# The last six column tiles of an output projection, split by halves of the tokens

## The chip, the cores and the metric

One Trainium2 chip, one of its cores. The metric is device microseconds from the start to the end of one execution. The kernel before was run three times on the chip; a further execution of it was recorded by the hardware profiler, and all rows below are from that one.

## The reference, cut to what matters

Two layers of an encoder over 512 tokens and 16 meta tokens (528 in all), width 2048. Layer 0 is attention, layer 1 gated linear attention. Each layer normalises its input, mixes, projects back to 2048, normalises again and adds the result to its input:

```
h = concat(meta, x)                                  # 528 x 2048
for i in 0, 1:
    y = rmsnorm(h, pre_norm[i])
    y = mixer_i(y, w_in[i], ...) @ w_out[i]          # gated outputs x w_out
    h = h + rmsnorm(y, post_norm[i])
return h[:, 16:]
```

The change is in the passage from layer 0 to layer 1: the product with `w_out[0]`, the norm of its result, the addition to `h`, the norm before layer 1 and the first product with `w_in[1]`.

## The kernel before

All activations are feature-major: 16 blocks k of 128 features, on partitions, by 528 tokens. The tokens are cut into two halves of 264 (HALVES). Float32 products are made in three passes of float32r: each operand is kept as a high part and the rest (`uh` and `ul` for activations, `whi` and `wlo` for weights), and `three` (lines 153 to 156) issues high x high, low x high, high x low.

**Weights.** `weights` (lines 143 to 151) fetches one unit: a DMA of 512 KB into `wraw` on SP's queue (line 149), a cast into `whi` on ACT (line 131) and a subtraction into `wlo` on DVE (line 132), the last two called the cast and the split here. `wraw` has two buffers, `whi` and `wlo` three each. A unit of `w_out` is 8 blocks k by 128 columns. The split of a unit frees its `wraw` buffer, and the last product with it frees its `whi` and `wlo`.

**Output projection.** `project` (lines 158 to 169) makes one column tile m of 128 columns: it fetches two units, and for each half of the tokens runs all 16 k, 48 products of 264 columns, and calls `evac`. Tiles 0 and 1 are made earlier; the loop over m = 2 to 15 makes the others. `evac` calls `squares` (lines 601 to 610): ACT writes `hs[m]` (line 602) and the square of the result (line 607), POOL adds the squares into `acc` (line 609). Behind the last tile's half, `mean_rsqrt` (lines 617 to 623) sums `acc` over partitions with TensorE (line 621), DVE makes mean and epsilon (line 622), ACT the reciprocal root (lines 135, 136) into `r0`.

**Residual step.** `residual(k, a, b)` (lines 625 to 639) fetches the layer's input `h0` by DMA on SP's queue (line 628), multiplies `hs[k]` by `r0` on DVE (630), adds `h0` on DVE for even k and on POOL for odd k (631), and splits the sum times the next norm's weight into `uh` (ACT, 632) and `ul` (DVE, 633). ACT squares it (638) and POOL adds the square to `acc` (639). It overwrites the gated outputs in `uh` and `ul`, so it may only begin for a half when all 16 column tiles of that half are made. For 264 tokens an even k takes 3 instructions on DVE and 1 on POOL, an odd k 2 and 2, so both together 5 and 3 (k = 0 has no line 639).

**First product of layer 1.** `group` (lines 171 to 188) makes two column tiles of `w_in[1]` for both halves at once, with k outermost. The first `halves` of k go by the first half of the tokens, then by the second, the others with both. Before the products of a k, `low_rank` (lines 650 to 663) issues the next residual step (`ahead`), the products `plr` (lines 652, 653), and, when the second half is there, four transposes of `hs[k]` into a PSUM tile `ht` (line 659), a copy of it on ACT into `hb` (line 661) and a DMA of `hb` (line 662). `ht` has one buffer for even k and one for odd k.

**Order.** The program writes the instructions in the order of the calls; a clock object `clk` places side work (`clk.after`, `clk.drive`) among the products by an estimated time. The framework then orders each engine's queue by itself, with weights pulled ahead (`high_priority(400)`). Each engine takes its queue strictly in order.

Of the kernel before, what the change touches and what calls it, by code (L numbers as in the profile page):

```python
# [19 lines left out]
P = 128  # L20
# [18 lines left out]
class Clock:  # L39
    """Order of emission: main steps advance the time, events run when it has come."""  # L40
# [42 lines left out]
def hybrid_encoder(  # L83
# [42 lines left out]
    # the activations of both layers and their gated outputs, feature-major, in two parts  # L126
# [31 lines left out]
    def project(src, c0, parts, evac, last_k=None):  # L158
        """One column tile of a projection: all of k for one part of the tokens, then for the next."""
        ws = [weights(src[:, k0:k0 + 8, c0:c0 + P]) for k0 in (0, 8)]  # L160
        for a, b in parts:
            ps = ps_p.tile([P, 512], F32, tag="pp", name="pp")[:, :b - a]
            for k in range(KT):
                wh, wl = ws[k // 8]
                three(ps, wh[:, k % 8], wl[:, k % 8], k, a, b, k == 0, k == KT - 1)
                clk.step(3 * (b - a + 7) / 2400)
                if last_k and (a, b) == parts[-1]:
                    last_k(k)
            evac(ps, a, b)

    def group(srcs, accs, extra, ahead=AHEAD, halves=0, units=None):
        """Several column tiles side by side, k outermost; the first of k by halves of the tokens, if asked."""
# [22 lines left out]
    # ======== layer 0: attention ========  # L195
# [10 lines left out]
    def take(wcol):  # L206
        """Evacuation of one q or k head: w * x and the squares."""
# [33 lines left out]
    def qk_tiles():  # L241
        kh = wk.tile([P, T], F32R, tag="kh", name="kh")
        kl = wk.tile([P, T], F32R, tag="kl", name="kl")
        # two heads' queries: real 0, meta 0, meta 1, real 1
# [107 lines left out]
    # per-token sums of squares: the norm as a column, and along the tokens  # L352
# [179 lines left out]
    # the output projection starts on the heads that are there  # L532
# [49 lines left out]
    # low-rank gate weights: the down-projection as columns [f hi, b hi, f lo, b lo] from multiples of 32,  # L582
    # the up-projections as rows [hi, lo, hi] against the inputs' rows [hi, hi, lo]
# [41 lines left out]
    def residual(k, a, b):  # L625
        if a == 0:
            h0s[k] = t2.tile([P, T], F32, tag="h0", name="h0", bufs=6)
            nc.sync.dma_start(out=h0s[k], in_=h0_d[k])
        h, hi = hs[k][:, a:b], uh[:, k, a:b]
        V.tensor_tensor(h, h, r0[:, a:b], op=ALU.mult)  # L630
        (G if k % 2 else V).tensor_tensor(h, h, h0s[k][:, a:b], op=ALU.add)
# [32 lines left out]
    def evac(ps, a, b):  # L664
        sq = squares(m, ps, a, b)
        if m == KT - 1:
            if a == 0:
                clk.after(1.5, lambda: mean_rsqrt(r0, [acc[:, a:b], sq], a, b))
                clk.after(2.5, lambda: ahead(NA))
            else:  # L670
                clk.after(0.9, lambda: mean_rsqrt(r0, [acc[:, a:b], sq], a, b))

    NA, NB = 2, 6
    h0s = {}
    tasks = [(k, a, b) for a, b in HALVES for k in range(NB)] + [(k, 0, T) for k in range(NB, KT)]
# [6 lines left out]
    for m in range(2, KT):  # L682
        project(w_out0, m * P, HALVES, evac)

# [30 lines left out]
    # ======== layer 1: gated linear attention ========  # L715
# [9 lines left out]
    # masks over a diagonal block, keys on partitions: forward j <= i, backward j > i  # L725
# [20 lines left out]
    def gates(h):  # L746
# [23 lines left out]
        # references of the key blocks, plus and minus, with the gate's 1/16  # L770
# [7 lines left out]
    def decayed(src, b, cc, j, sgn, c, n, what):  # L778
        """hi/lo of src * exp(sgn * (b - c_j) / 16) over n columns from c, both key tiles."""
# [145 lines left out]
    # the gated outputs come back for the output projection, and its norm's weights  # L925
# [43 lines left out]
    # ======== output projection, token-major, and the last residual ========  # L969
    def token_group(n, banks, on_k=None, evac=None):  # L970
        """512 columns of all token tiles, which end one after another if they are to be finished here."""
# [99 lines left out]
```

## Time and profile before

| | |
|---|---|
| median of 3 runs | 1826.01 us (1825.46 to 1826.07) |
| span of the profiled execution | 1825.2 us |
| the same above or below the median of the runs | 0.8 us below |
| PE busy | 1784.4 us, 98% |
| DVE busy | 1014.2 us, 56% |
| ACT busy | 892.9 us, 49% |
| POOL busy | 202.5 us, 11% |

The profile gives, for the execution that it recorded, the span from the first to the last instruction; a time around it is not shown, so the 0.8 us are taken to lie around it. PE is TensorE's products, PEld its weight loads, DVE is VectorE, ACT ScalarE, POOL GpSimd, SP the queue from which most DMAs are issued. The shares are means over the whole span; the passage that the change touches is about 130 us of it.

### The profile page before, as it was taken

How to read it: one execution, taken by the hardware profiler on the slowest of the kernel's cores; microseconds unless marked ns; L12 is line 12 of the kernel's file. 1: busy time of each engine (PE TensorE's matmuls, PEld its weight loads, DVE VectorE, ACT ScalarE, POOL GpSimd, SP SyncE). 2: the span in 40 equal slices, each digit the busy share in tenths (PEclk: the TensorE clock that was granted, in tenths of full speed). 3: DMA queues.
4: the chain of work that ended last, by engine and by line, in shares of the span. 5: the costliest groups of instructions: out<-in, count | busy, mean ns of one | idle time of the engine just before them, and what ended most of it. 6: DMA issues, size and time to landing. Idle time of an engine off the chain costs nothing.

```text
span 1825.2 us, 31789 instructions
## 1 busy us (share of the span) xinstructions
PE 1784.4 (98%) x12825; PEld 1683.3 (92%) x12825; DVE 1014.2 (56%) x1941; ACT 892.9 (49%) x1835; POOL 202.5 (11%) x212
## 2 busy tenths in 40 slices
PE   8899999999999999999987999999999999999997
PEld 7899999999999999999987898998999899988886
DVE  5776665656565657622258475656456555654224
ACT  5555444454454544533245586556447455743221
POOL 2211111111111110211137000000000000000000
PEclk9999999999999999999998999999999999999999
DMA  8323232333223242633335323232232323434323
GB/s 266 106 59 82 82 88 85 93 85 88 83 87 93 81 120 76 185 93 93 93 88 163 87 72 89 83 82 82 81 93 80 84 87 92 134 116 172 94 92 127
DMA packets 264595, 184.22 MB, mean 101 GB/s; under 512 B 8108, under 2 KB 240112, under 8 KB 263920
## 3 DMA queue, kind: packets, MB, share of 16 engines
q1 hardware_dynamic: 259808, 165.78, 31.5%
q0 software_dynamic: 4640, 16.42, 2.5%
q8 instruction: 100, 1.64, 0.4%
q14 instruction: 47, 0.39, 0.1%
HBM read 156.03 MB, written 19.64 MB: 96 GB/s over the span
## 4 chain that ended last, share of the span: by engine, by line
PE 92%; DVE 3%; ACT 1%; DMA 1%; POOL 1%; issue 1%; SPq 0%; DVEq 0%; POOLq 0%; ACTq 0%
PE pp L154 22%; PE pp L156 22%; PE pp L155 22%; PE f L985 2%; PE f L983 2%; PE f L984 2%; PE pT L453 2%; PE s L434 1%; PE s L435 1%; PE s L436 1%; PE o L863 1%; PE o L862 1%; PE o L861 1%; PE o L474 1%; PE o L473 1%
## 5 line engine op out<-in xcount | busy, mean ns | idle before, releaser
L154 PE MATMUL pp<-uh,whi 128*128 128x264 f32 (+1 forms) x3072 | 927.4, 302 | 2.5 <-ACT uh L308 2.1
L156 PE MATMUL pp<-uh,wlo 128*128 128x264 f32 (+1 forms) x3072 | 916.4, 298 | 0.0
L155 PE MATMUL pp<-ul,whi 128*128 128x264 f32 (+1 forms) x3072 | 915.1, 298 | 0.7 <-DVE ul L309 0.7
L154 PEld LDWEIGHTS pp<-uh,whi 128*128 128x128 f32 x3072 | 578.5, 188 | 21.1 <-ACT uh L308 2.5
L155 PEld LDWEIGHTS pp<-ul,whi 128*128 128x128 f32 x3072 | 578.8, 188 | 16.9 <-DVE ul L309 1.2
L156 PEld LDWEIGHTS pp<-uh,wlo 128*128 128x128 f32 x3072 | 578.5, 188 | 16.2
L132 DVE TENSOR_TENSOR wlo<-wraw,whi 128x1024 fp32r<-128x1024 f32 x256 | 316.0, 1235 | 385.8 <-ACT whi L131 380.7
L131 ACT CAST whi<-wraw 128x1024 fp32r<-128x1024 f32 x256 | 267.7, 1047 | 416.1 <-PE pp L155 297.1
L443 ACT ACTIVATE pn<-s,mx 128x528 f32<-128x528 f32 (+1 forms) x72 | 50.4, 699 | 88.4 <-DVE mx L440 65.0
L985 PE MATMUL f<-whi,ul 128*128 128x512 f32 x192 | 75.6, 394 | 0.0
L983 PE MATMUL f<-whi,uh 128*128 128x512 f32 x192 | 75.5, 393 | 0.0
L984 PE MATMUL f<-wlo,uh 128*128 128x512 f32 x192 | 75.3, 392 | 0.0
L225 POOL TENSOR_TENSOR qw<-qw,cos 128x528 f32<-128x528 f32 x24 | 31.9, 1328 | 372.2 <-DMA qs<-qw 347.7
L888 POOL DMA_DIRECT2D og_d<-og x24 | 12.9, 545 | 486.8 <-DVE og L886 486.8
L439 DVE TENSOR_REDUCE mx<-s 128x1 f32<-128x528 f32 (+1 forms) x72 | 50.8, 705 | 18.5 <-PE s L436 17.3
L235 DVE TENSOR_TENSOR qw<-qw,qs 128x528 f32<-128x528 f32 x24 | 17.0, 708 | 60.0 <-POOL qs L226 60.0
L458 DVE TENSOR_TENSOR pl<-pT,ph 128x512 fp32r<-128x512 f32 (+1 forms) x80 | 47.4, 593 | 4.8 <-ACT ph L457 3.8
L457 ACT CAST ph<-pT 128x512 fp32r<-128x512 f32 (+1 forms) x80 | 40.7, 508 | 16.5 <-PE pT L453 10.4
L428 POOL TENSOR_TENSOR gs<-gs,gr 128x528 f32<-128x528 f32 x16 | 21.2, 1323 | 222.3 <-ACT gs L141 205.4
L984 PEld LDWEIGHTS f<-wlo,uh 128*128 128x128 f32 x192 | 36.1, 188 | 8.3
L985 PEld LDWEIGHTS f<-whi,ul 128*128 128x128 f32 x192 | 36.1, 188 | 8.3
L983 PEld LDWEIGHTS f<-whi,uh 128*128 128x128 f32 x192 | 36.1, 188 | 8.1
(306 smaller groups left out, 2743.2 us busy)
## 6 DMA issues: line engine op xcount, KB each, us to landing
wraw<-in_gla_w_in_dram SPq DMA_DIRECT2D x96, 512.0 KB, 3.9
wraw<-in_attn_w_in_dram SPq DMA_DIRECT2D x95, 512.0 KB, 4.1
wraw<-in_attn_w_out_dram SPq DMA_DIRECT2D x32, 512.0 KB, 3.9
wraw<-in_gla_w_out_dram SPq DMA_DIRECT2D x32, 512.0 KB, 3.8
qs<-qw SPq DMA_DIRECT2D x96, 66.0 KB, 3.0
h<-h_d SPq DMA_DIRECT2D x16, 264.0 KB, 3.8
h_d<-h POOLq DMA_DIRECT2D x16, 256.0 KB, 2.9
h_d<-hb SPq DMA_DIRECT2D x16, 256.0 KB, 3.1
```

What stands on the lines that cost most here:

```text
L131: A.copy(hi, src)
L132: V.tensor_tensor(lo, src, hi.bitcast(F32), op=ALU.subtract)
L154: PE.matmul(ps, wh, uh[:, k, a:b], start=first, stop=False)
L155: PE.matmul(ps, wh, ul[:, k, a:b], start=False, stop=False)
L156: PE.matmul(ps, wl, uh[:, k, a:b], start=False, stop=last)
L439: V.reduce_max(mx, s, axis=AX.XY)
L443: A.activation(pn[:, :T].rearrange("p (a b) -> p a b", a=2), s, AF.Exp, bias=mx, scale=SCALE, accum_out=sm)
L457: A.copy(ph[:, :, c:c + m], pt[:, :, qc:qc + m])
L458: V.tensor_tensor(pl[:, :, c:c + m], pt[:, :, qc:qc + m], ph[:, :, c:c + m].bitcast(F32), op=ALU.subtract)
L983: PE.matmul(ps, uh[:, k, ts], wh[:, kk], start=(k == 0), stop=False)
L984: PE.matmul(ps, uh[:, k, ts], wl[:, kk], start=False, stop=False)
L985: PE.matmul(ps, ul[:, k, ts], wh[:, kk], start=False, stop=(k == KT - 1))
```

## The change

Tiles 2 to 9 are made as before. Tiles 10 to 15 are made for the first half of the tokens, one after the other, and then for the second half, so each of their weights is fetched and split twice. When the first half's mean is there, a side task issues the 16 residual steps of the first half, one every 2.0 us of the clock, beside the products of the second half. The 16 residual steps of the second half are issued from `group`, whose first 10 k (6 before) go by halves. `h0` is fetched by half (132 KB into 8 buffers) and no longer whole (264 KB into 6). Comments and some docstrings are gone as well.

```diff
     def residual(k, a, b):
-        if a == 0:
-            h0s[k] = t2.tile([P, T], F32, tag="h0", name="h0", bufs=6)
-            nc.sync.dma_start(out=h0s[k], in_=h0_d[k])
+        h0 = t2.tile([P, HALF], F32, tag="h0", name="h0", bufs=8)
+        nc.sync.dma_start(out=h0, in_=h0_d[k][:, a:b])
...
-        (G if k % 2 else V).tensor_tensor(h, h, h0s[k][:, a:b], op=ALU.add)
+        (G if k % 2 else V).tensor_tensor(h, h, h0, op=ALU.add)
...
-                clk.after(2.5, lambda: ahead(NA))
+                clk.after(3.0, lambda: side.append(clk.drive(residuals(KT))))
...
-    NA, NB = 2, 6
-    h0s = {}
-    tasks = [(k, a, b) for a, b in HALVES for k in range(NB)] + [(k, 0, T) for k in range(NB, KT)]
+    TAIL, NB = 6, 10
+    side = []
+    tasks = [(k, a, b) for a, b in HALVES for k in range(KT)]
...
+    def residuals(n):
+        for _ in range(n):
+            ahead(1)
+            yield 2.0
+
-    for m in range(2, KT):
+    for m in range(2, KT - TAIL):
         project(w_out0, m * P, HALVES, evac)
+    for part in HALVES:
+        for m in range(KT - TAIL, KT):
+            project(w_out0, m * P, (part,), evac)
+    clk.finish(*side)
```

From line 628 on the line numbers of the two kernels differ by one: line 630 of before is 629 of the change, 631 is 630, 633 is 632, 661 is 660.

**VectorE, at the last tiles of the projection.** `wlo` is a unit's split, `r0` the first half's mean, lines 630 to 633 the residual steps; the number behind `h` is k. Before, with the splits of the last tile's units and of the group's first ones:

```order
L132 TENSOR_TENSOR wlo_11506<-wraw_11504,whi_11505 128x1024
L622 TENSOR_SCALAR r0_9785<-ssq_11446 128x264
L630 TENSOR_TENSOR h0_9768<-h0_9768,r0_9785 128x264
L630 TENSOR_TENSOR h1_9769<-h1_9769,r0_9785 128x264
L631 TENSOR_TENSOR h0_9768<-h0_9768,h0_11461 128x264
L132 TENSOR_TENSOR wlo_11586<-wraw_11584,whi_11585 128x1024
L633 SCALAR_TENSOR_TENSOR ul_88<-h0_9768,cols_85,uh_87 128x264
L633 SCALAR_TENSOR_TENSOR ul_88<-h1_9769,cols_85,uh_87 128x264
L630 TENSOR_TENSOR h2_9770<-h2_9770,r0_9785 128x264
L630 TENSOR_TENSOR h3_9771<-h3_9771,r0_9785 128x264
L631 TENSOR_TENSOR h2_9770<-h2_9770,h0_11510 128x264
L132 TENSOR_TENSOR wlo_11828<-wraw_11826,whi_11827 128x1024
```

With the change, where `wlo_11254` and `wlo_11260` are the two units of tile 11 for the second half, and `wlo_11337` the first of tile 12:

```order
L132 TENSOR_TENSOR wlo_11254<-wraw_11252,whi_11253 128x1024
L622 TENSOR_SCALAR r0_9785<-ssq_11193 128x264
L629 TENSOR_TENSOR h0_9768<-h0_9768,r0_9785 128x264
L629 TENSOR_TENSOR h1_9769<-h1_9769,r0_9785 128x264
L630 TENSOR_TENSOR h0_9768<-h0_9768,h0_11211 128x264
L132 TENSOR_TENSOR wlo_11260<-wraw_11258,whi_11259 128x1024
L632 SCALAR_TENSOR_TENSOR ul_88<-h0_9768,cols_85,uh_87 128x264
L632 SCALAR_TENSOR_TENSOR ul_88<-h1_9769,cols_85,uh_87 128x264
L629 TENSOR_TENSOR h2_9770<-h2_9770,r0_9785 128x264
L629 TENSOR_TENSOR h3_9771<-h3_9771,r0_9785 128x264
L630 TENSOR_TENSOR h2_9770<-h2_9770,h0_11280 128x264
L132 TENSOR_TENSOR wlo_11337<-wraw_11335,whi_11336 128x1024
```

The residual steps of the first half have moved from ahead of the splits of `w_in[1]` to ahead of those of `w_out`'s last tiles. Between one split and the next stand five of their instructions, for two steps; this goes on through eight splits, `wlo_11260` to `wlo_11613`.

**ScalarE, in the group.** Lines 632 (631 with the change) and 638 (637) are residual steps; `hb` are the copies of the transposes. Before, the three copies are those of k = 9, 10 and 11:

```order
L632 ACTIVATE uh_87<-h12_9780,cols_85 128x528
L638 ACTIVATE sq1_11904<-h12_9780 128x528
L661 COPY hb_11883<-ht_11878 128x512
L632 ACTIVATE uh_87<-h13_9781,cols_85 128x528
L638 ACTIVATE sq1_11937<-h13_9781 128x528
L632 ACTIVATE uh_87<-h14_9782,cols_85 128x528
L638 ACTIVATE sq1_11976<-h14_9782 128x528
L661 COPY hb_11916<-ht_11911 128x512
L632 ACTIVATE uh_87<-h15_9783,cols_85 128x528
L638 ACTIVATE sq1_12009<-h15_9783 128x528
L661 COPY hb_11949<-ht_11944 128x512
```

With the change they are those of k = 2, 3, 4, 5 and 6, where `whi_12157` is the group's last unit and `whi_12276` the first of the projection behind it:

```order
L660 COPY hb_11960<-ht_11955 128x512
L131 CAST whi_12157<-wraw_12156 128x1024
L631 ACTIVATE uh_87<-h13_9781,cols_85 128x264
L637 ACTIVATE sq1_11975<-h13_9781 128x264
L660 COPY hb_11985<-ht_11980 128x512
L631 ACTIVATE uh_87<-h14_9782,cols_85 128x264
L637 ACTIVATE sq1_12000<-h14_9782 128x264
L660 COPY hb_12010<-ht_12005 128x512
L631 ACTIVATE uh_87<-h15_9783,cols_85 128x264
L637 ACTIVATE sq1_12025<-h15_9783 128x264
L660 COPY hb_12035<-ht_12030 128x512
L131 CAST whi_12276<-wraw_12275 128x1024
```

The copies have moved back against the residual steps: behind the last step stood the copy of k = 11, now it is that of k = 5. The first copy, of k = 0, stands behind the step of k = 9 with the change, and behind that of k = 2 before.

Elsewhere the order between casts and evacuations is as it was: the last evacuation of the second half (`h15`) stands on ScalarE behind the cast of the group's third unit in both kernels.

## Rows read from the trace of the kernel before

**Rows 1.** The page's head: the span, and of each engine the busy time, its share of the span and the instructions.

```profile
span 1825.2 us, 31789 instructions
PE 1784.4 (98%) x12825; PEld 1683.3 (92%) x12825; DVE 1014.2 (56%) x1941; ACT 892.9 (49%) x1835; POOL 202.5 (11%) x212
```

**Rows 2.** Busy time of each engine by stretches (from:to, its length, then PE, PEld, DVE, ACT and POOL busy with their instructions, the granted clock, the share of the DMA engines, GB/s). The first stretch is in the output projection, the others from the first residual step to the last, and the whole of `group`.

```profile
880.00:920.00 40.00, 40.00 (x332) 40.00 (x331) 9.27 (x8) 13.32 (x22) 5.66 (x6) 1.00 0.31 87
939.90:943.50 3.60, 3.33 (x25) 2.92 (x25) 3.54 (x7) 2.74 (x7) 1.03 (x2) 1.00 0.00 0
943.50:948.60 5.10, 3.63 (x26) 3.29 (x26) 5.10 (x8) 2.91 (x7) 3.66 (x4) 1.00 0.47 125
948.90:963.50 14.60, 10.68 (x80) 9.46 (x79) 14.60 (x24) 10.15 (x24) 10.07 (x11) 1.00 0.63 184
942.60:1005.10 62.50, 46.50 (x325) 43.30 (x326) 55.67 (x58) 34.72 (x67) 44.63 (x35) 0.92 0.52 149
```

**Rows 3.** What PE waited for between 930 and 1006 us: who waited for whom, us in total, times, longest.

```profile
PE ht L659 <- ACT hb L661: 8.2, 4, 4.4
PE plr L653 <- DVE ul L633: 6.0, 7, 1.5
PE plr L652 <- ACT uh L632: 1.5, 1, 1.5
```

**Rows 4.** ACT's instructions in order of time (start and duration in us; in brackets the idle time before and what ended it): a cast, the evacuations of tiles 14 and 15, the first half's reciprocal root, and the copy of the transposes of k = 10.

```profile
915.32 1.05 ACT L131 CAST whi<-wraw 128x1024 fp32r<-128x1024 f32 x1 [2.06 <-PE pp L155]
...
924.17 0.48 ACT L602 ACTIVATE h<-pp,cols 128x264 f32<-128x264 f32 x1 [4.22 <-PE pp L156]
...
935.84 0.48 ACT L602 ACTIVATE h<-pp,cols 128x264 f32<-128x264 f32 x1 [4.22 <-PE pp L156]
...
944.11 0.47 ACT L602 ACTIVATE h<-pp,cols 128x264 f32<-128x264 f32 x1
...
993.05 0.56 ACT L661 COPY hb<-ht 128x512 f32<-128x512 f32 x1
```

**Rows 5.** PE in order of time: the first product of `group`, the transposes of k = 12 to 15, and the sum that ends it.

```profile
942.70 0.39 PE L652 MATMUL plr<-uh,wl 128*128 128x264 f32 x1
...
993.66 1.12 PE L659 MATMUL ht<-ident,h 128*128 128x128 f32 x4 [2.88 <-ACT hb L661]
...
998.10 0.89 PE L659 MATMUL ht<-ident,h 128*128 128x128 f32 x4
...
1000.79 0.60 PE L659 MATMUL ht<-ident,h 128*128 128x128 f32 x4
...
1003.18 0.60 PE L659 MATMUL ht<-ident,h 128*128 128x128 f32 x4
...
1005.08 0.61 PE L621 MATMUL ssq<-acc,ones 128*128 128x264 f32 x2
```

**Rows 6.** DVE in order of time: two splits in the projection, and the residual steps from the first one on (x2 are two instructions that overlap).

```profile
916.39 1.23 DVE L132 TENSOR_TENSOR wlo<-wraw,whi 128x1024 fp32r<-128x1024 f32 x1 [7.53 <-ACT whi L131]
...
930.99 1.23 DVE L132 TENSOR_TENSOR wlo<-wraw,whi 128x1024 fp32r<-128x1024 f32 x1 [1.69 <-ACT whi L131]
...
938.57 0.43 DVE L622 TENSOR_SCALAR r<-ssq 128x264 f32<-128x264 f32 x1 [6.36 <-PE ssq L621]
939.96 0.78 DVE L630 TENSOR_TENSOR h<-h,r 128x264 f32<-128x264 f32 x2 [0.95 <-ACT r L136]
940.65 0.43 DVE L631 TENSOR_TENSOR h<-h,h 128x264 f32<-128x264 f32 x1
940.99 1.77 DVE L132 TENSOR_TENSOR wlo<-wraw,whi 128x1024 fp32r<-128x1024 f32 x1
942.69 0.88 DVE L633 SCALAR_TENSOR_TENSOR ul<-h,cols,uh 128x264 fp32r<-128x264 f32 x2
943.50 1.33 DVE L630 TENSOR_TENSOR h<-h,r 128x264 f32<-128x264 f32 x2
...
948.57 0.42 DVE L622 TENSOR_SCALAR r<-ssq 128x264 f32<-128x264 f32 x1
948.91 0.76 DVE L630 TENSOR_TENSOR h<-h,r 128x264 f32<-128x264 f32 x2
...
963.38 0.70 DVE L630 TENSOR_TENSOR h<-h,r 128x528 f32<-128x528 f32 x1
964.00 0.76 DVE L633 SCALAR_TENSOR_TENSOR ul<-h,cols,uh 128x528 fp32r<-128x528 f32 x1
```

**Rows 7.** SP's queue: the first load of a unit behind the split above.

```profile
917.65 0.37 SPq L149 DMA_DIRECT2D wraw<-in_attn_w_out_dram  x1
```

**Rows 8.** The loads of line 149 from 800 to 925 us, from issue to landing.

```profile
DMA to landing us min/median/max: 3.8/3.9/4.1
```

**Rows 9.** POOL's instructions on 264 columns between 938.5 and 997.1 us, grouped by form (busy us, mean ns; idle before, releasers).

```profile
L639 POOL TENSOR_TENSOR acc<-acc,sq 128x264 f32<-128x264 f32 x10 | 9.2, 925 | 3.0 <-ACT sq L638 2.7
...
L631 POOL TENSOR_TENSOR h<-h,h 128x264 f32<-128x264 f32 x6 | 5.6, 936 | 12.6 <-DVE h L630 12.6
```

**Rows 10.** POOL in order of time, in the projection: the addition of squares, beside an idle DVE and beside a split.

```profile
925.01 0.76 POOL L609 TENSOR_TENSOR acc<-acc,sq 128x264 f32<-128x264 f32 x1 [3.85 <-ACT sq L607]
931.70 1.13 POOL L609 TENSOR_TENSOR acc<-acc,sq 128x264 f32<-128x264 f32 x1 [5.93 <-ACT sq L607]
```

## The prediction, made before the changed kernel ran

> **What bounds the kernel now.** I read the page's head first: PE is busy for 98% of 1825.2 us, DVE for 56% [rows 1]. So only a stretch in which PE waits can give time back. The table by stretches finds it: in the projection PE is busy 40.00 of 40 us and DVE 9.27; in `group` PE is busy 46.50 of 62.50 us and DVE 55.67 [rows 2]. PE's own list of waits names the two things it waited for there: the residual steps' `ul` and `uh` (7.5 us) and ACT's copies of the transposes (8.2 us) [rows 3]. From 939.9 to 963.5 us DVE is busy without a break [rows 2], so DVE sets the pace of this passage and PE follows it.
>
> How much could be had? A half of a tile takes (935.84 - 924.17) / 2 = 5.83 us [rows 4]. With everything there, a k of `group` takes 1003.18 - 1000.79 = 2.39 us, so 16 take 38.2 [rows 5], where 62.4 passed (942.70 to 1005.08). The change aims at these 24 us, by moving half of DVE's residual work beside products during which DVE is idle. I follow it on one time axis: 0 is the start of tile 10, which before is 935.84 - 11 x 5.83 = 871.7 us. Before, the group's end then lies at 1005.1 - 871.7 = **133.4**.
>
> **Part 1, the first half's six tiles (0 to 35.0): nothing lost, but the reserve goes.** 6 x 5.83 = 35.0 us, as before. Each tile now needs two units per 5.83 us, before per 11.67: 12 more loads, casts and splits. A `wraw` buffer turns round in: split's end to the next issue 0.03 (916.39 + 1.23 to 917.65) [rows 6, 7], landing 3.9 [rows 8], cast 1.05 and 0.02 to the split (915.32 to 916.39) [rows 4, 6], split 1.23, some 0.03 of waking: 6.25 us for two units, which PE eats in 5.83. The first such unit is split at 2.4 (a `whi` buffer comes free at 0) and needed at 5.83; twelve units later 2.4 + 6 x 6.25 = 39.9 stands against 40.8. So PE does not starve; ACT and DVE are idle enough to cover the 12 x (1.05 + 1.23) us (DVE 9.27 of 40 [rows 2]). But the mean of the first half is queued behind this: on DVE `r0` stands behind `wlo_11254`, the unit split at 39.9. From `r0`'s start to the first residual step 939.96 - 938.57 = 1.39 us pass [rows 6], so the steps begin at 41.3, 6.3 us into the second half's products. PE, whose `ssq` product waits for the square behind the same cast on ACT, stands still for some 2.5 us.
>
> **Part 2, the second half's six tiles.** The order on DVE is five residual instructions, then one split, through eight splits. The cost of such a round is the number that decides. Undisturbed, an instruction of 264 columns starts 940.99 - 940.65 = 0.34, say 0.35 us after the one before, one of 528 columns 0.62, a split 1.23 - 0.07 = 1.16 [rows 6]: a round is 5 x 0.35 + 1.16 = 2.9 us. Beside POOL it is longer: from 948.91 to 963.38 stand 20 instructions of 264 and 2 of 528 columns, 8.2 us undisturbed, 14.5 in fact, with POOL busy 10.07 [rows 2, 6]. So each us of POOL costs DVE (14.5 - 8.2) / 10.07, about 0.6 us. A round has 3.5 POOL instructions (one line 631, two line 639, half a line 609) of 0.93 us [rows 9], 3.3 us: 2.9 + 0.6 x 3.3 = **4.9 us**. The two rounds of the trace are 3.54 us, with POOL busy 1.03, and 5.07 with 3.66 [rows 2, 6]; the second is the one that looks like the steady state. PE eats a unit in 2.92 us, so it waits 2 us in each round.
>
> The first split ends 942.69 - 939.96 = 2.73 us after the first step [rows 6]: 44.0. Seven rounds more: 44.0 + 7 x 4.9 = 78.3; call it S, the split of the last tile's first unit. The second follows at S + 2.9 and PE ends the tile at S + 5.85 = 84.2, where 71.0 (with 1.0 for `ssq`) would do: **13 us lost here**. SP's `h0` loads (32 of 132 KB for 16 of 264) stand between the weights' loads; each waits for a step that is over before the split its neighbour waits for, so I count nothing. POOL is busy 3.3 of 4.9 us and holds nobody up.
>
> **Between the halves.** The group's weights could not run ahead, since their buffers hang on these late splits: units at S + 6.3 (one turn of 6.25), S + 9.2, S + 12.6. On ACT the last evacuation stands behind the third unit's cast, on DVE `r0` behind its split. So the second half's steps begin at S + 12.6 + 1.39 = S + 14.0; the gain of part 2 is spent a second time in idling DVE.
>
> **Part 3, the group.** 16 steps are 40 x 0.35 + one split 1.16 + 0.6 x (24 x 0.93) = 28.6 us: DVE ends at S + 42.6. PE cannot follow closely: transposes of k need the PSUM tile of k - 2, and on ACT the copy of k = 0 stands behind the step of k = 9, that of k = 5 behind the step of k = 15. So PE stops at the transposes of k = 2 and is let go one k at a time; it passes those of k = 7 at about S + 42.6. Left are some 16 products (1.9 us), then 6 x 2.39 + 0.7 for k = 10 to 15: S + 59.6. Before, only 1005.08 - 993.66 = 11.4 us were left when the copy of k = 10 let PE go at 993.62 [rows 4, 5].
>
> After a wait PE also ran at half clock: the transposes of k = 12 came after 2.88 us of waiting, and this k took 998.10 - 993.66 = 4.44 us and not 2.39 [rows 5] (granted clock 0.92 over `group` [rows 2]). I take 1.0 of these 2.05 us, for PE waits in pieces here; the ends are 0 and 2.05.
>
> **The sum:** 78.3 + 59.6 + 1.0 = 138.9 against 133.4: **+5.5 us**. Made against the span of 1825.2 us, this is 1830.7; with the 0.8 us by which the median of the runs lies above it, **1831.5 us**.
>
> Bounds: the round between 4.3 (mean of the two seen) and 5.6 (below): -4.2 to +4.7. The start of the steps at 39.1 (4.1 into part 2, as before: 935.84 to 939.96) and not 41.3: -2.2. The clock: -1.0 to +1.05. A landing of 4.1 for 3.9 [rows 8] over seven turns: +1.4.
>
> **Rivals.** *Full turns.* If DVE and POOL shut each other out entirely, a round is 2.9 + 3.5 x 0.76 (POOL's time alone [rows 10]) = 5.6 us and the second half's steps 15.2 + 24 x 0.76 = 33.4: 7 x 0.7 + 4.8 = 9.7 us more, 1841. For it: the second round took 5.07. Against it: 14.5 us held 8.2 + 10.07. Chance 0.12. The Trainium skill, SBUF — State Buffer, "Who interferes with whom", states this: a DVE instruction with two SBUF inputs and a GpSimd one that reads SBUF exclude each other for a whole instruction. By that rule alone the round of 5.6 and a sum of 1841 would hold; the trace agrees on who collides and shows 0.6 of the price.
>
> *POOL pays, not DVE* (the other side). A split at 930.99 took its usual 1.23 us, and POOL's addition beside it 1.13 for 0.76 [rows 6, 10]: here the loser was POOL. If the queues fall so that DVE pays only 0.3 per us of POOL, a round is 3.9, the steps of part 3 take 21.9: -7.0 - 6.7, total 8 us faster than before, 1818. It decides from about 0.4 down. Against it: no stretch of residual steps in the trace shows under 0.6. Chance 0.16.
>
> *Level.* Rounds near 4.3 and steps that begin at 39.1 give 5.5 - 4.2 - 2.2 = -0.9, 1825. Chance 0.24: the casts of part 1 need only land a little earlier, and the first round was 3.54.
>
> *Order without effect.* That the steps do not lie beside the second half's products is excluded by DVE's order. That all 24 us are had needs rounds under 2.92 us, which DVE undisturbed just makes: I give it no share of its own.
>
> **How the numbers follow.** A measurement of this kernel can tell 0.2%, 3.65 us, from no change. Forecast +5.5 with 0.48, full turns 0.12: slower 0.60. Level 0.24. Faster 0.16. The range leaves out half of the fast rival and the far end of the slow one: 1820 to 1841.
>
> **What would show it.** Right: DVE busy throughout part 2 with a split every 4.9 us; PE waiting for `wlo` on the products of tiles 12 to 15, some 2 us each; some 14 us between the last tile's first split and the second half's first step, with DVE nearly idle; PE's list led by `ht` behind `hb`, with one wait of about 6 us at k = 2, and about 17 us of products after DVE's last step. Wrong: no wait for `wlo` (then part 2 costs 36 us and the kernel is faster), a split every 3.5 us, or a PE that follows the second half's steps closely, ending within 5 us of DVE.

## The result, and the profile after

The changed kernel takes 1833.91 us (median of 4 runs, 1833.12 to 1835.16) against 1825.93 us of the kernel before on the same chip: a ratio of 1.0039, interval 1.0027 to 1.0051, which is 7.1 us at 1826 us. (The medians lie 8.0 us apart; what follows goes by the ratio.) Forecast were 1831.5 us and +5.5 us, with 0.60 on slower. The sign, the mechanism and nearly every step held; one term, the tail behind VectorE's last step, was about 2 us too small.

The page's head of the changed kernel answers to [rows 1]. PE has the same 12825 products. DVE has 37 instructions more, twelve splits that are now made twice and 25 from steps that were whole and are now halves, and 18 us more, mostly for the splits.

```profile
span 1832.6 us, 31973 instructions
PE 1788.5 (98%) x12825; PEld 1687.7 (92%) x12825; DVE 1032.2 (56%) x1978; ACT 907.3 (50%) x1867; POOL 201.6 (11%) x227
```

The next view answers to [rows 2], with the same columns: from the first half's `r0` to the last split of `w_in[1]` ahead of the second half's `r0`, then the second half's steps on DVE, then from the end of these to the group's end.

```profile
912.50:962.60 50.10, 41.43 (x289) 39.77 (x287) 43.31 (x53) 29.09 (x58) 27.32 (x28) 0.90 0.59 167
964.20:992.50 28.30, 22.75 (x161) 22.13 (x161) 28.23 (x41) 17.62 (x41) 21.37 (x25) 0.84 0.35 98
992.50:1013.40 20.90, 17.91 (x146) 17.07 (x144) 2.49 (x3) 7.23 (x12) 1.16 (x4) 1.00 0.73 206
```

DVE is busy for 43.31 of 50.10 us in the first of them, where it was 9.27 of 40 before, and PE stands in all three. What PE waited for between 860 and 1020 us answers to [rows 3]:

```profile
PE ht L658 <- ACT hb L660: 8.5, 4, 3.6
PE ssq L621 <- ACT sq L607: 5.6, 2, 3.0
PE pp L156 <- DVE wlo L132: 5.0, 4, 1.9
PE ssq L621 <- POOL acc L609: 0.6, 1, 0.6
PE ssq L621 <- DVE r1row L622: 0.6, 1, 0.6
```

The waits for `ul` and `uh` are gone (7.5 us before). The splits' `wlo` and the squares behind the casts stand in their place, and the waits for `hb` are as large as before (8.2).

DVE in order of time answers to [rows 6]: the first half's `r` and first step, the first and the last of the eight splits of part 2, three of the four splits behind them, the second half's `r` and first step, two instructions of line 630, the last instructions of the steps, and the row behind the group.

```profile
912.55 0.43 DVE L622 TENSOR_SCALAR r<-ssq 128x264 f32<-128x264 f32 x1 [0.47 <-PE ssq L621]
913.93 0.78 DVE L629 TENSOR_TENSOR h<-h,r 128x264 f32<-128x264 f32 x2 [0.94 <-ACT r L136]
915.39 1.35 DVE L132 TENSOR_TENSOR wlo<-wraw,whi 128x1024 fp32r<-128x1024 f32 x1 [0.34 <-ACT whi L131]
...
948.29 1.77 DVE L132 TENSOR_TENSOR wlo<-wraw,whi 128x1024 fp32r<-128x1024 f32 x1
...
955.34 1.22 DVE L132 TENSOR_TENSOR wlo<-wraw,whi 128x1024 fp32r<-128x1024 f32 x1 [1.78 <-ACT whi L131]
958.73 1.23 DVE L132 TENSOR_TENSOR wlo<-wraw,whi 128x1024 fp32r<-128x1024 f32 x1 [2.17 <-ACT whi L131]
961.46 1.23 DVE L132 TENSOR_TENSOR wlo<-wraw,whi 128x1024 fp32r<-128x1024 f32 x1 [1.50 <-ACT whi L131]
962.89 0.43 DVE L622 TENSOR_SCALAR r<-ssq 128x264 f32<-128x264 f32 x1 [0.21 <-PE ssq L621]
964.27 0.78 DVE L629 TENSOR_TENSOR h<-h,r 128x264 f32<-128x264 f32 x2 [0.95 <-ACT r L136]
...
977.78 0.97 DVE L630 TENSOR_TENSOR h<-h,h 128x264 f32<-128x264 f32 x1
...
979.97 0.42 DVE L630 TENSOR_TENSOR h<-h,h 128x264 f32<-128x264 f32 x1
...
990.21 2.32 DVE L632 SCALAR_TENSOR_TENSOR ul<-h,cols,uh 128x264 fp32r<-128x264 f32 x3
...
1013.42 0.43 DVE L622 TENSOR_SCALAR r1row<-ssq 128x264 f32<-128x264 f32 x1 [9.87 <-PE ssq L621]
```

On the prediction's axis (0 at 871.7 us): the first step begins at 42.2 (forecast 41.3). Eight splits end from 916.66 to 949.98 (the next instruction starts then), so a round takes 33.32 / 7 = 4.76 us (forecast 4.9), and S is 78.3, as forecast. The second half's first step comes at S + 14.3 (14.0), with DVE idle before each of the last three splits; DVE ends at S + 42.5 (42.6). `r1row` comes 7.7 us later than before (1005.72 there).

The same rows show what POOL costs DVE as a step. Beside POOL, an instruction of line 630 takes 0.97 us and not 0.42, a split 1.77 and not 1.23: most of the stretched instructions in this stretch are longer by 0.50 to 0.55 us, whatever their own length, and POOL's addition takes 0.76 us alone [rows 10]. With 3.5 additions a round is 2.9 + 3.5 x 0.55 = 4.8 us.

Two traces don't reach the changed tiles at the same time. The last evacuation of tile 9, just ahead of them, in the kernel before, in the changed kernel and in the run below that halves with few steps:

```profile
872.50 0.48 ACT L602 ACTIVATE h<-pp,cols 128x264 f32<-128x264 f32 x1
872.67 0.47 ACT L602 ACTIVATE h<-pp,cols 128x264 f32<-128x264 f32 x1
874.88 0.48 ACT L602 ACTIVATE h<-pp,cols 128x264 f32<-128x264 f32 x1
```

For the two kernels the 0.2 us can be left out. From this evacuation to `r1row` pass 133.2 us before and 140.8 in the changed kernel, 7.5 more; below, this stretch is called the passage. Its length is a second measure of a run, from one execution.

The end is a different matter. ACT's copies of the transposes:

```profile
995.26 0.58 ACT L660 COPY hb<-ht 128x512 f32<-128x512 f32 x1 [2.32 <-DMA h_d<-hb]
999.21 0.59 ACT L660 COPY hb<-ht 128x512 f32<-128x512 f32 x1 [2.57 <-DMA h_d<-hb]
1005.31 0.59 ACT L660 COPY hb<-ht 128x512 f32<-128x512 f32 x1 [1.62 <-DMA h_d<-hb]
1010.19 1.25 ACT L660 COPY hb<-ht 128x512 f32<-128x512 f32 x2 [4.29 <-DMA h_d<-hb]
```

and SP's queue, from which the stores of these copies are issued:

```profile
990.32 0.37 SPq L149 DMA_DIRECT2D wraw<-in_gla_w_in_dram  x1
990.78 1.08 SPq L661 DMA_DIRECT2D h_d<-hb  x2
994.23 0.37 SPq L149 DMA_DIRECT2D wraw<-in_gla_w_in_dram  x1
995.88 7.30 SPq L661 DMA_DIRECT2D h_d<-hb  x5
1003.58 0.37 SPq L149 DMA_DIRECT2D wraw<-in_gla_w_in_dram  x1
```

A copy needs one of two `hb` buffers, a buffer comes free when its store has landed, and the store may stand on SP behind a weight load that waits for a split: the load of 990.32 us was issued when the split of 988.52 us ended (1.77 us later), and the store behind it at 990.78 us. The prediction had ACT's copies and PE's transposes in its tail, but not the stores.

### The profile page after: what moved, and what is told of

It is laid out like the page before. It is cut to its first block, busy times and chain, and to the rows that moved or that the text cites. A ratio compares the mean times of both kernels' runs of the same rounds, so it can differ in the third digit from the quotient of the medians.

```text
span 1832.6 us, 31973 instructions
## 1 busy us (share of the span) xinstructions
PE 1788.5 (98%) x12825; PEld 1687.7 (92%) x12825; DVE 1032.2 (56%) x1978; ACT 907.3 (50%) x1867; POOL 201.6 (11%) x227
## 4 chain that ended last, share of the span: by engine, by line
PE 88%; DVE 5%; DMA 3%; ACT 2%; issue 1%; POOL 0%; SPq 0%; DVEq 0%; ACTq 0%; POOLq 0%
PE pp L154 21%; PE pp L156 21%; PE pp L155 21%; PE f L995 2%; PE f L993 2%; PE f L994 2%; PE pT L453 2%; DVE wlo L132 1%; DMA wraw<-in_attn_w_out_dram 1%; ACT whi L131 1%; DVE ul L632 1%; PE s L434 1%; PE s L435 1%; PE s L436 1%; PE o L473 1%
## 5 line engine op out<-in xcount | busy, mean ns | idle before, releaser
L154 PEld LDWEIGHTS pp<-uh,whi 128*128 128x128 f32 x3072 | 580.8, 189 | 20.7 <-ACT uh L308 2.0
L132 DVE TENSOR_TENSOR wlo<-wraw,whi 128x1024 fp32r<-128x1024 f32 x268 | 333.9, 1246 | 377.4 <-ACT whi L131 372.1
L131 ACT CAST whi<-wraw 128x1024 fp32r<-128x1024 f32 x268 | 280.3, 1047 | 430.7 <-PE pp L155 279.3
```

Of the source, the lines that this page charges most:

```text
L131: A.copy(hi, src)
L132: V.tensor_tensor(lo, src, hi.bitcast(F32), op=ALU.subtract)
L154: PE.matmul(ps, wh, uh[:, k, a:b], start=first, stop=False)
```

## The experiments

Times are given against the kernel before, run on the same chip beside each kernel; where a run is set against the changed kernel, the difference of the two ratios is taken, times 1828 us. Each ratio's interval reaches about 0.001 to either side, so such a difference is known to 2.5 to 3 us either way.

**A third buffer for the raw weights**, from tile 10 to the group, on the changed kernel (`third[0]()` is true for every third unit):

```diff
...
-            raw = wpool.tile([P, 1024], F32, tag="wraw", name="wraw", bufs=2)
+            if third and third[0]() :
+                raw = t2.tile([P, 1024], F32, tag="rawx", name="wraw", bufs=1)
+            else:
+                raw = wpool.tile([P, 1024], F32, tag="wraw", name="wraw", bufs=2)
...
```

> The changed kernel, with a third wraw buffer for the units from tile 10 to the end of group; the order of all instructions stays as it was. Theory (the late means come from the two-buffer ring of loads): the first half's steps begin at 911.0 us of the trace and not at 913.9, the rounds of part 2 stay at 4.8 us, and from the split of the last tile's first unit to the second half's first step pass 11 us and not 14.3. In all 6 us less than the changed kernel: 1828 (1826 to 1830). Rival (fetching the weights twice costs by its traffic and its casts and splits, however they are buffered): 1834, within 1 us.

Ratio 1.0009 (1.0001 to 1.0018): 5.5 us below the changed kernel; the passage takes 135.0 us, 5.8 less. DVE's `r` of both halves (the line numbers are 5 higher here):

```profile
909.25 0.43 DVE L627 TENSOR_SCALAR r<-ssq 128x264 f32<-128x264 f32 x1 [0.55 <-PE ssq L626]
...
956.81 0.43 DVE L627 TENSOR_SCALAR r<-ssq 128x264 f32<-128x264 f32 x1 [0.20 <-PE ssq L626]
```

The first is 3.3 us earlier than in the changed kernel, the second 6.1. The eight splits end from 913.45 to 946.79 us, so the round is 4.76 us as in the changed kernel: the ring prices the starts of the two halves and not the rounds. The loads, casts and splits are as many as before this edit, so the 5.5 us are not the price of the traffic itself, and the rival falls.

**No transposes**: ACT copies 512 columns of `hs[k]` itself into `hb`, and the store writes those; the four transposes of each k are left out. On the changed kernel, then on the kernel before:

```diff
...
-        for t in range(4):
-            PE.transpose(ps[:, t * P:(t + 1) * P], hs[k][:, t * P:(t + 1) * P], ident)
...
-        A.copy(hb, ps)
+        A.copy(hb, hs[k][:, :512])
```

> The changed kernel without the transposes of group: ACT copies hs itself into hb, so the stored block is not transposed; copies and stores stay. Theory (PE is held in group by the copies that stand behind the residual steps): 5.6 us of transposes go, and some 10 us of waiting with them; PE ends about 5 us after DVE's last step. 1818 (1815 to 1822). Rival (PE is late in group through its clock or through late weights): only the 5.6 us go, 1828.

> The same taken from the kernel before. Theory: there the copies hold PE for only about 2 us behind DVE's last step, so 6 to 8 us go, 1819 (1817 to 1821), and the changed kernel without transposes is level with it or ahead by some 2 us, where it was 8 behind. Rival: the distance of 8 us stays.

Ratios 0.9989 (0.9980 to 0.9998) and 0.9964 (0.9952 to 0.9976): 9.1 us below the changed kernel and 6.6 us below the kernel before. The control came out as expected, the other fell short by 7 us. The two kernels are 4.6 us apart without transposes, where the theory had them level or the changed one ahead, and its rival 8 apart. The trace of the changed kernel's version shows both halves of the matter. PE does follow DVE: the sum of squares on PE, which ends the group, comes at 1000.43 us, 3.7 us after DVE's last residual instruction. But ACT's reciprocal root of it comes only at 1009.93 us, behind these copies:

```profile
996.67 1.37 ACT L656 COPY hb<-h 128x512 f32<-128x512 f32 x2 [1.18 <-DMA h_d<-hb]
1000.60 1.36 ACT L656 COPY hb<-h 128x512 f32<-128x512 f32 x2 [1.61 <-DMA h_d<-hb]
1004.24 0.62 ACT L656 COPY hb<-h 128x512 f32<-128x512 f32 x1 [2.28 <-DMA h_d<-hb]
1007.77 1.30 ACT L656 COPY hb<-h 128x512 f32<-128x512 f32 x2 [2.91 <-DMA h_d<-hb]
1009.93 0.41 ACT L135 ACTIVATE r1row<-r1row 128x264 f32<-128x264 f32 x1
```

So it is at the transposes that PE is held, as the prediction has it, but what the hold costs this run doesn't give, since another bound lies close behind it: the copies' waits for their stores.

**No running sum of squares on POOL**: line 638 of the changed kernel is left out.

```diff
-            G.tensor_tensor(acc[:, a:b], acc[:, a:b], sq, op=ALU.add)
+            pass
```

> The changed kernel without POOL's addition of the squares of the residual steps (line 638), so the next norm's sum holds only k = 0. POOL keeps 1.5 of its 3.5 instructions per round. Theory (DVE pays 0.6 us per us of POOL): a round of part 2 is 2.9 + 0.6 x 1.4 = 3.75 us where it was 4.76. Full turns: 2.9 + 1.5 x 0.76 = 4.05, and were the same rule right for the whole kernel it would have been 5.6 there. Rival (the round is the chain from DVE over POOL and ACT back to DVE, not the collision): 4.5 or more, since line 638 is on no such chain. In time the theory gives 1818 (1813 to 1824).

Ratio 0.9992 (0.9982 to 1.0002), 8.6 us below the changed kernel, with 16 expected. The rounds are as expected: the eight splits end from 918.19 to 944.48 us, 26.29 / 7 = 3.76 us. Two POOL instructions of 0.93 us [rows 9] fewer took 1.00 us from the round, 0.54 us of DVE per us of POOL; the forecast took 0.6. DVE's last residual instruction ends at 981.6 us, 11 earlier (12 within the passage, which this trace reaches 1.3 us later), but `r1row` comes only at 1004.11: two of ACT's copies wait 5.32 and 3.88 us for stores in the tail. Part of what DVE gained was given back there, at the bound that the run without transposes showed.

**Four `hb` buffers**, to test that bound alone:

```diff
-        hb = t2.tile([P, 512], F32, tag="hb", name="hb")
+        hb = t2.tile([P, 512], F32, tag="hb", name="hb", bufs=4)
```

> The changed kernel with four buffers instead of two for the transposed copies `hb`, which its stores read. Nothing is left out and no other line differs. Theory (the tail that the prediction made too short is the ring of the two `hb` buffers: from 995 us on ScalarE's copies stand 1.6 to 4.3 us each for a store of an earlier copy, and PE's transposes stand for the copies): the last residual instruction on VectorE still ends near 992, the waits of the copies for stores fall from 10.8 us in sum to under 3, and the row `r1row` of the first half comes near 1010.5 instead of 1013.4, so the time is 2 to 3 us below the changed kernel's. Rival (the tail is the products and transposes that PE still owes when VectorE ends, and the waits of the copies lie beside them): `r1row` stays within 0.7 us of 1013.4 and the time with it.

Ratio 1.0028 (1.0018 to 1.0038), 2.0 us below the changed kernel; the intervals of the two overlap, so the trace has to carry this. The passage takes 138.4 us, 2.3 less: `r1row` comes at 1010.90 instead of 1013.42, while DVE's steps and the splits lie within 0.5 us of those of the changed kernel. One wait for a store above 0.2 us is left, of 1.73 us, and in the tail PE stands for nothing:

```profile
992.50:1010.90 18.40, 18.35 (x152) 18.07 (x151) 2.82 (x3) 7.82 (x12) 1.50 (x5) 1.00 0.86 244
```

18.35 of 18.40 us busy, where the changed kernel has 17.91 of 20.90. PE's own work behind DVE's last step takes the 18 us that the forecast had there (17, and 1.0 for the clock); the 2.5 us above it go with the ring of the two `hb` buffers.

**The stores issued by ScalarE** instead of SyncE, on the changed kernel and on the kernel before:

```diff
-        nc.sync.dma_start(out=h1_d[:, :, k * P:(k + 1) * P].rearrange("t p c -> p t c"),
+        nc.scalar.dma_start(out=h1_d[:, :, k * P:(k + 1) * P].rearrange("t p c -> p t c"),
```

> The changed kernel with the stores of `hb` issued by ScalarE instead of SyncE; nothing is left out. On SyncE such a store stands behind weight loads that wait for a buffer (994.23 and 1003.58 us in the changed kernel's trace). Theory (the stores come late because of where they are queued): the copies' waits for stores become shorter than 1.5 us each with two buffers too, and the time falls 2 to 3 us below the changed kernel's, as with four buffers. Rival 1 (the stores' own landing time fills the ring, wherever they are queued): the waits stay and the time is within 1 us of the changed kernel's. Rival 2 (a store that ScalarE issues holds up the copies and squares behind it): 1 to 3 us slower than the changed kernel.

> The kernel before with the stores of `hb` issued by ScalarE instead of SyncE; nothing is left out. It is the control of the run with that edit on the changed kernel. Theory (late stores are a cost of the changed kernel's tail, in which the steps of the second half follow each other closely on VectorE with half the work each, so that copies and stores come closer together): within 1 us of the kernel before. Rival (the late stores cost both kernels the same, and explain nothing of their distance): 2 to 3 us faster than the kernel before.

Ratios 1.0050 (1.0038 to 1.0063) and 1.0005 (0.9997 to 1.0014): no gain in either; against the changed kernel 2 us more, with intervals that overlap. The theory on the queue falls for the changed kernel. The stores go out as soon as the copy is there, and the copies wait as before:

```profile
999.08 0.59 ACT L660 COPY hb<-ht 128x512 f32<-128x512 f32 x1 [2.41 <-DMA h_d<-hb]
...
1002.67 0.37 ACTq L661 DMA_DIRECT2D h_d<-hb  x1
...
1008.45 0.59 ACT L660 COPY hb<-ht 128x512 f32<-128x512 f32 x1 [4.28 <-DMA h_d<-hb]
```

So the place behind the weight loads, which SP's queue shows so plainly, is not what sets the ring's pace: with two buffers the stores' own time to land does it as well, and only more buffers helped. The store of 1002.67 us, for which the copy of 1008.45 waits, landed 5.69 us after its issue, where the median store takes 2.5; in the changed kernel the one issued on SP at 1004.04 took 6.05. Beside the store of 1002.67 a weight load of 512 KB was under way (issued at 1001.89 us); whether it made the store late was not tried. The kernel before says less as a control: its copies were queued anew (three behind the last `uh` where five stood), and PE waited 12.2 us for `ul` there, and no longer for `hb`.

**The halving with few steps beside it**: six of the sixteen first-half steps beside the second half's products, the other ten k after the last tile and of whole rows, as before, with `h0` fetched whole again. (Two of the six are issued beside the products, the others by `group`; in DVE's queue all six lie between the splits.)

```diff
...
-                clk.after(3.0, lambda: side.append(clk.drive(residuals(KT))))
+                clk.after(2.5, lambda: ahead(2))
...
-    TAIL, NB = 6, 10
+    TAIL, NB = 6, 6
...
-    tasks = [(k, a, b) for a, b in HALVES for k in range(KT)]
+    tasks = [(k, a, b) for a, b in HALVES for k in range(NB)] + [(k, 0, T) for k in range(NB, KT)]
```

> The halving alone, with few steps beside it: the last six tiles go by halves of the tokens as in the changed kernel, with the same second loading and splitting of their weights, but only the first six of the sixteen first-half steps lie beside the second half's products, and ten tiles' steps are of whole rows after the last tile, as before the change (h0 in whole rows, six buffers). Nothing is left out. Theory (VectorE's rounds of 4.76 us each, in which two steps lie between two splits, set the time): three rounds, then splits at the ring's pace of 3.1 us, so the last tile's first split ends near 942.5 us instead of 950.0, the second half's first step begins 14 us behind it at about 957, VectorE's steps end near 998, and the time is 1 to 4 us above the kernel before. Rival (the cost is the halving itself, that is twice the loads, casts and splits and PE at less than its pace there, whatever lies beside it): the splits end as late as in the changed kernel, near 950, and the time is 7 to 9 us above the kernel before.

Ratio 1.0026 (1.0017 to 1.0036): 4.8 us above the kernel before. After the steps are used up, the splits come freely at the ring's pace, behind ACT's casts:

```profile
926.61 1.77 DVE L132 TENSOR_TENSOR wlo<-wraw,whi 128x1024 fp32r<-128x1024 f32 x1
929.85 1.62 DVE L132 TENSOR_TENSOR wlo<-wraw,whi 128x1024 fp32r<-128x1024 f32 x1
933.46 1.22 DVE L132 TENSOR_TENSOR wlo<-wraw,whi 128x1024 fp32r<-128x1024 f32 x1 [1.99 <-ACT whi L131]
936.51 1.23 DVE L132 TENSOR_TENSOR wlo<-wraw,whi 128x1024 fp32r<-128x1024 f32 x1 [1.82 <-ACT whi L131]
```

The eighth starts at 942.96 us where it was 948.29, and the second half's `r` at 956.96 where it was 962.89; as this trace reaches the passage 2.2 us later, that is 7.5 and 8.1 us earlier. The rival (splits as late as in the changed kernel) falls. The time is 0.8 us above the upper end that the theory gave: the steps ended at 1002.1, 999.9 without the 2.2 us, and not near 998. The passage takes 137.0 us, 3.8 less than in the changed kernel and 3.8 more than before; the ratios, 2.4 us apart, don't tell this run from the changed kernel. So with three such rounds in place of eight the halving still loses 4.8 us; with none it was not run.

**POOL's additions of the residual steps on DVE**, on the changed kernel and on the kernel before:

```diff
-        (G if k % 2 else V).tensor_tensor(h, h, h0, op=ALU.add)
+        V.tensor_tensor(h, h, h0, op=ALU.add)
...
-            G.tensor_tensor(acc[:, a:b], acc[:, a:b], sq, op=ALU.add)
+            V.tensor_tensor(acc[:, a:b], acc[:, a:b], sq, op=ALU.add)
```

> The changed kernel with the residual steps' additions that GpSimd did (h0 of every second step, and the running sum of squares) done by VectorE; nothing is left out. Theory (a GpSimd instruction of 0.93 to 1.1 us costs VectorE about 0.6 us per us, and the same addition on VectorE alone costs 0.35): a round with one split and two steps falls from 4.76 to at most 4.1 us, though VectorE has three instructions more in it, the splits come at about the ring's 3.1 to 3.5 us in the scheduler's order (five instructions between two splits), the second half's first step begins near 957 to 960 instead of 964.3, VectorE ends near 983 to 987, and the time is 7 to 11 us below the changed kernel's, which is level with the kernel before or up to 4 us below. Rival 1 (VectorE is simply full: the number of its instructions sets the round): the round grows by three times 0.35 to about 5.8 us and the time is 10 to 16 us above the changed kernel's. Rival 2 (VectorE then waits for ScalarE's squares in its own queue): time within 2 us of the changed kernel's.

> The kernel before with the same additions moved from GpSimd to VectorE; nothing is left out. It is the control of that edit. Theory: VectorE's 48 us of steps behind the last tile (948.9 to 997) get some 5 us shorter, and the copies and stores of `hb` give part of that back: 3 to 5 us below the kernel before. If only the changed kernel gains, the interference is a cost of the steps beside the splits alone; if both gain the same, it explains nothing of their distance.

Ratios 0.9950 (0.9938 to 0.9963) and 0.9914 (0.9900 to 0.9927): 16 us below the changed kernel and 15.7 us below the kernel before, far more than expected. In the changed kernel's version hardly an instruction on DVE is stretched any more, though DVE has more of them:

```profile
938.93 1.21 DVE L132 TENSOR_TENSOR wlo<-wraw,whi 128x1024 fp32r<-128x1024 f32 x1
940.07 0.98 DVE L632 SCALAR_TENSOR_TENSOR ul<-h,cols,uh 128x264 fp32r<-128x264 f32 x1
940.98 0.42 DVE L638 TENSOR_TENSOR acc<-acc,sq 128x264 f32<-128x264 f32 x1
941.32 0.76 DVE L630 TENSOR_TENSOR h<-h,h 128x264 f32<-128x264 f32 x2
942.01 0.42 DVE L629 TENSOR_TENSOR h<-h,r 128x264 f32<-128x264 f32 x1
942.48 1.23 DVE L132 TENSOR_TENSOR wlo<-wraw,whi 128x1024 fp32r<-128x1024 f32 x1
```

A split takes 1.2 and not 1.77 us (the one 0.98 stands beside one of the additions of line 609 that stayed on POOL), and the first eight splits come every 3.44 us (914.87 to 938.93 us). The second half's first step begins at 956.23 us, 8.0 earlier. The passage takes 124.9 us, 15.9 less. So from that step to the end 8 us more are gained, and these are not all POOL's: with its estimates changed, the framework also sorts ACT's queue anew, and puts the first copy of transposes behind the fifth `uh` of the second half where it stood behind the ninth (the step of k = 9). In the kernel before it is the same: DVE's steps end 8 us earlier, `r1row` comes 15 us earlier, and behind the last `uh` stands one copy where five stood. PE then follows DVE more closely. The two shares of the second gain were not told apart in either kernel.

The stretches of the second half's steps, of the changed kernel with this edit:

```profile
956.20:985.90 29.70, 28.79 (x228) 28.08 (x228) 26.10 (x66) 20.37 (x47) 1.85 (x5) 0.96 0.55 157
```

and of the whole group, of the kernel before with it:

```profile
940.00:991.00 51.00, 48.41 (x352) 43.27 (x351) 48.39 (x92) 36.84 (x71) 3.19 (x5) 1.00 0.65 188
```

PE is busy nearly throughout, at a granted clock of 0.96 and 1.00, where the group before had 46.50 of 62.50 at 0.92 [rows 2]. Since both kernels gain the same within the intervals, what this edit takes away is a price that both pay. POOL beside DVE sets the length of the rounds, but not the distance between the two kernels.

**The two rings together**, a third raw buffer and three `hb` buffers, without and with POOL's additions on DVE (the edits above, with `bufs=3` for `hb`):

> The changed kernel with a third buffer for the raw weights from tile 10 to the group, and three `hb` buffers; nothing is left out. Theory (the two rings act in different stretches, so their prices add): 5.5 and 2 to 3 us, that is 7.5 to 8.5 below the changed kernel, within 2 us of the kernel before; `r1row` near 1005. Rival (the group's end is held by one of them at a time): 5 to 6 us below the changed kernel, as with the third raw buffer alone.

> The changed kernel with all three edits: third raw weight buffer, three `hb` buffers, and GpSimd's additions of the residual steps on VectorE; nothing is left out. Theory: the steps beside the second half cost little more than the products then, and the time is 4 to 9 us below the kernel before. Rival (VectorE's load ahead of the group's end no longer counts and PE's own products and the clock set it): level with the run that has the additions on VectorE alone, within 1.5 us.

Ratios 0.9990 (0.9981 to 0.9999) and 0.9887 (0.9873 to 0.9900). The first is 9.0 us below the changed kernel, about what the two rings gave one by one (5.5 and 2.0), and level with the kernel before by the bound of 0.2%. `r1row` comes at 1004.79 us; the passage takes 132.9 us, 7.9 less than in the changed kernel. The second is 20.7 us below the kernel before and the fastest of all: 1807.32 us (median of 4) against 1827.63, and against 1812.45 of the kernel before with the additions on DVE (their intervals just touch). `r1row` comes at 986.84 us, and of PE's waits from 860 to 1020 us one is left:

```profile
PE ssq L626 <- ACT sq L612: 2.8, 1, 2.8
```

So the new order with its two rings is worth some 4 to 5 us once POOL doesn't stand beside it: 4.9 by the ratios (0.9914 to 0.9887), 3.7 by the passage (118.3 and 114.6 us). The two rings were not enlarged in the kernel before, and ACT's queue is sorted differently there, so how much of this is the order alone stays open. With POOL's additions on DVE, PE waits there for 1.8 us in all between 930 and 1006 us, which leaves little for a larger ring to give; that is argued and was not run.

## Why the prediction was right, step by step

*What bounds the kernel.* Right: DVE's steps and ACT's copies. That POOL's share could be had cheaply could have been read: the 0.6 us per us of POOL stood in the text, while an addition on DVE itself takes 0.35 us. With these additions on DVE and ACT's queue sorted anew, the kernel before gained 15.7 us.

*Part 1.* Right in its place, 0.9 us small: the first step came at 42.2 for 41.3. The ring turned in 6.3 us for two units (splits 3.1 to 3.2 us apart) for 6.25. PE stood 2.58 us at `ssq`, 2.5 forecast. With a third buffer this term fell away, as it should.

*Part 2.* Right: rounds of 4.76 us for 4.9, S at 78.3 for 78.3; that the two agree to the digit is luck, as the start, 0.9 us late, and the seven rounds, each 0.14 short, cancel. PE's waits for `wlo` are 5.0 us in four and not 2 us in each round, because PE ran part of the stretch at the lower level of its clock (granted 0.50 from 911.9 to 915.2 us, behind a wait of 2.58 us, and 0.60 from 935.7 to 940, behind one of 1.89) and took longer for the same products.

*Between the halves.* Right: 14.3 us for 14.0, though DVE was not nearly idle in it: it was busy for 7.67 of 14.2 us, with the last steps' instructions and four splits. In the run with a third raw buffer it was 11.4.

*Part 3.* DVE's 28 us were right. PE was held at k = 2 and 3 for 3.6 and 2.0 us, and not once at k = 2 for 6, and it passed the transposes of k = 7 at 991.8 us, close to the forecast's S + 42.6 (992.5). Here the step failed that gives the end, S + 59.6 and 1.0 for the clock: the sum of squares that ends the group came at 1012.78 us, S + 62.8. The prediction said "on ACT the copy of k = 0 stands behind the step of k = 9", which held, and then counted products and transposes alone. The copies' two buffers and their stores were left out. With four buffers PE is busy 18.35 of 18.40 us there, close to the forecast's 18.0; with two it takes 20.90. That the 18.0 fit is in part luck. In the run with four buffers the clock granted is 1.00 there, so the 1.0 taken for it bought something else: from 992.5 us to the transposes of k = 10 pass 3.9 us, for 1.9 counted, and from there to the last sum 13.9, for 15.0. In the changed kernel the term was 2.2 us too small, and that is the whole difference in the sum: 78.3 + 62.8 - 133.4 = 7.7 us for 5.5.

*The clock.* 1.0 us was taken; the tail itself ran at 1.00, while the steps ran at 0.84 (0.51 from 980 to 985 us, around PE's wait of 2.0 us at k = 3). No run settles this term by itself.

*Rivals.* Full turns (0.12) is out: rounds of 4.76, not 5.6, and without two POOL additions 3.76, as DVE loses 0.50 to 0.55 us to an addition and not 0.76. The Trainium skill, SBUF — State Buffer, "Who interferes with whom", has the shared ports locked for a whole instruction, by which the two additions of 0.76 us would have taken 1.52 from a round; the runs show 1.00. That POOL pays and not DVE (0.16) is out by the same numbers: 0.54 per us, and the limit was 0.4. Level (0.24) needed rounds near 4.3 and steps that begin at 39.1; neither came.

## What to carry to other kernels

Work placed beside a stretch lives on the stretch's reserve: before filling idle time, work out the turn of each ring that feeds it (here 6.3 us for two units that PE eats in 5.83) and of each ring that drains what comes out, as it will be the next bound when the first is gone. One more buffer in each of two rings gave back 9.0 us here (7.9 by the passage), all of the 7.1 that the change had cost. And before moving work to hide it, see what makes it long: three additions per pair of steps, taken off POOL, gave twice what the new order had lost, in part by the new sorting of ACT's queue that came with them. An edit of one engine's work can sort another's queue anew, so read the queues of both runs before a time is put down to the edit.

## What the runs showed that was not expected

DVE is faster with more work. With POOL's three additions in a round taken over, DVE's splits took 1.22 us for 1.77, and eight of them came every 3.44 us for 4.76. In the kernel before, the same two lines gave 15.7 us, with ACT's queue sorted anew.

A store's place in its queue did not matter in the changed kernel: issued without delay by ScalarE, a store still held a copy for 4.28 us, and the time did not fall. With four buffers one wait of 1.73 us was left.
